# A transformer block in fp32 on one core: half of V made in the opening from unnormalised x, no V product inside attention, and the value differences made by GpSimd

## The chip, the core and the metric

The kernel runs on one core of a Trainium2 chip. The core has five engines that run side by side, each through its own list of instructions in order: TensorE (PE in the profile, its weight loads PEld), VectorE (DVE), ScalarE (ACT), GpSimd (POOL) and SyncE (SP), whose list here holds only transfers (SPq). ScalarE's list holds transfers too (ACTq). An instruction waits for the semaphores of those it depends on, and everything behind it on that engine waits with it. The metric is the device time of one execution in microseconds (us).

## The reference

The program is one layer (`DEPTH = 1`) on `x` of 1024 tokens by 1024 channels, all float32:

```python
mod = silu(c) @ ada_w + ada_b                 # six vectors of 1024: sh1, sc1, g1, sh2, sc2, g2
h = rmsnorm(x, ln1_g) * (1 + sc1) + sh1
q, k, v, cb, cc, cx, ga, gb = split(h @ w_in) # 8 sections of 1024 columns
q, k = rmsnorm per head of 64; 16 heads
y_a = stick_breaking_attention(q, k, v)       # strictly causal, no softmax
y_b = cb * causal_dwconv3(cc * cx)
merged = sigmoid(ga) * (y_a @ w_branch_a) + sigmoid(gb) * (y_b @ w_branch_b)
x = x + g1 * (merged @ w_out)
h = rmsnorm(x, ln2_g) * (1 + sc2) + sh2
x = x + g2 * ((silu(h @ w_gate) * (h @ w_up)) @ w_down)   # hidden width 2816
```

In the attention a weight is A[t,s] = sigmoid(z_ts) times the product over s<j<t of (1 - sigmoid(z_tj)). With P[t,s] the running product from the right, A[t,s] = P[t,s+1] - P[t,s], so the output is a sum of P against differences of neighbouring rows of v, plus the last row of v in the query block. That is how the kernel computes it: a scan for P, and products with v[s-1] - v[s].

For the change two facts matter. The norm of a token is one number r_t per row of x, so x's row can be multiplied by a weight matrix first and by r_t afterwards. And h = r_t * a * x + sh1 with a = ln1_g * (1 + sc1) per channel; the shift adds the same row sh1 @ W to every token's v. In differences of neighbouring rows that row cancels. It has to be put back only in the first difference and in the "last row" term.

## The kernel before

TensorE's matmuls take fp32r operands. For fp32 accuracy each operand is split into a high part (ScalarE copies it to fp32r) and a low part (VectorE subtracts), and each product is three matmuls: high x high, high x low, low x high. A "token" product (`mm_tok`) makes 128 tokens by 512 columns from 8 slices of 128 channels, that is 24 matmuls of 512 columns into one of 8 PSUM banks. Tiles in PSUM pools are called `pj` and `tr`, in later stages `e`.

The stages in order:

1. **Opening** (lines 165 to 350). The eight row tiles of `x` (`xq`) are loaded, squared and summed (odd ones by VectorE, even ones by ScalarE) and turned into r_t (`rstd_of`). TensorE meanwhile multiplies `xq` by the identity into a scratch bank (line 262, `warm`). The modulation's first two sections are dot products of 1024-wide rows of `ada` with silu(c), by VectorE (`mod_sum`, line 250, two per slice of 128 channels). r_t is spread over partitions by 8 small matmuls (`bcast`, line 279). Then, slice by slice, transposed `x` (`xts`) is normalised (`norm_x`, line 287), shifted and split (`make_hi` line 292, `make_lo` line 296), the weight split (`split_hi`, `split_lo`), and `real(k, ...)` issues slice k's 24 matmuls for 8 token tiles, which hold all 8 banks. This makes the first half of V (heads 0 to 7), stored in `d_v[0]`.
2. **K** (from line 430): 16 token tiles, with the factors of a Strassen scheme being made beside it (`factors`, `more`). Tiles `wpa` hold six 1024-wide weights; `raw` has two buffers.
3. **Gates** (from line 647): five sections by Strassen products. GpSimd makes sums of weights there.
4. **Attention** (from line 723). 16 heads by 8 query blocks give 128 steps. In each step TensorE makes scores (`z`, line 808), ScalarE the sigmoid, VectorE the scan (line 818); two steps later TensorE transposes (line 832), ScalarE and VectorE split (`ath` line 835, `atl` line 836), and three steps later TensorE multiplies by the value differences (`o`, lines 847 and 848). `att_dv` makes those for the next head: a difference on VectorE (tile `vb`), a high part on ScalarE, a low part on VectorE (tile `vt`). Between the steps TensorE runs fillers, paced by nominal costs (`F_Z`, `F_T`, `FILL`, `HEAD`): first the second half of V (lines 927 to 929, 2 x 8 tiles of 128 tokens by 256 columns), then the section cb (`C` below) and the product with `w_branch_b`, whose result VectorE multiplies by sigmoid(gb) (tile `mb`, line 982; sigmoid(gb) in tile `sgi`). `HEAD` = 16 pieces of filler come ahead of the first step. TensorE's instructions are chained in program order from the first step on, and so are attention's on VectorE.
5. **w_branch_a** (from line 1057): `ya` is loaded through `yr` (two buffers), split and multiplied; VectorE adds `mb`.
6. The output projection, the second norm, the FFN by Strassen products, as before and after.

In the opening every engine keeps program order, SyncE too (`in_order`); elsewhere a planner orders each engine's list, with attention's steps at high priority. The lines of the value difference:

```python
        if part == 0:
            tt(nc.vector, dv, dv, va[:, :, cs], ALU.subtract)
            return
        vt = vts[h] = bp.tile([P, KT, P], F32R, tag="vt", bufs=2, name=nm("vt"))
        nc.scalar.activation(vt[:, :, :DH], dv, AF.Copy)
        tt(nc.vector, vt[:, :, DH:], dv, vt[:, :, :DH].bitcast(F32), ALU.subtract)
```

Of the kernel before, what the change touches and what calls it, by code (L numbers as in the profile page):

```python
# [17 lines left out]
P = 128  # L18
# [12 lines left out]
def block_kernel(tc, x, x_t, cols, ada_1, ada_2, ada_row, w_q, w_kv, w_v1, w_cg, w_a, w_b, w_o, w_g, w_u, w_d, out):  # L31
# [38 lines left out]
    d_v = [drp.tile([n, P + 1, KT, P], F32, name=f"d_v{n}_{e}") for e, n in enumerate((4, 2, 2))]  # L70
# [5 lines left out]
    d_mb = drp.tile([KT, P, T], F32, name="d_mb")  # L76
    d_g = [drp.tile([P, D], F32, name=f"d_g{e}") for e in range(2)]
# [15 lines left out]
    nc.scalar.activation(one, one, AF.Sigmoid)  # L93
# [75 lines left out]
    sa_ = ExitStack()  # L169
    adp = sa_.enter_context(tc.tile_pool(name="adp", bufs=1, side="right", reuse_waits="tile"))  # L170
# [9 lines left out]
    xqs = [bigp.tile([P, 4, D], F32, tag="big", bufs=4, name=nm("xq")) for n in range(2)]  # L180
    xq = [xqs[i // 4][:, i % 4, :] for i in range(8)]
    rs = sp.tile([P, T], F32, name="rs")
    cab = sp.tile([P, D], F32, name="cab")
    nc.scalar.dma_start(cab, ada_row[0:1, :].broadcast_to([P, D]))
    hh = [big() for n in range(2)]
    junk = [h_[:, :2, :].rearrange("p a t -> p (a t)") for h_ in hh]

    def load_xq(i0_, i1_):
        for i in range(i0_, i1_):
            nc.sync.dma_start(xq[i], x[i * P:(i + 1) * P, :])  # L190
# [3 lines left out]

    wq = []
    MC0, MC = 3, 2
    ads = []

    def load_ada(e):
        ad = adp.tile([P, 2, D], F32, tag="ada", bufs=2, name=nm("ada")) if e % 3 < 2 else sp.tile(  # L200
            [P, 2, D], F32, tag="ada", bufs=1, name=nm("ada"))
        nc.sync.dma_start(ad, ada_1[e])
        ads.append(ad)
# [26 lines left out]

    load_xq(0, 4)
    load_ada(0)
    load_xq(4, 8)
    load_x(0)
    load_wq(0)
    load_ada(1)
    load_x(1)
    load_ada(2)
    load_x(2)
    load_wq(1)  # L240
    load_x(3)
# [4 lines left out]
    def mod_sum(e):  # L246

        msum = sp.tile([P, 2], F32, tag="msum", bufs=2, name=nm("msum"))
        for m in range(2):
            nc.vector.tensor_tensor_reduce(out=ads[e][:, m], in0=ads[e][:, m], in1=cab, scale=1.0, scalar=0.0, op0=ALU.mult,  # L250
                                           op1=ALU.add, accum_out=msum[:, m:m + 1])
# [84 lines left out]
    for k in range(KT - 1):  # L336
# [11 lines left out]
        if k % 2 == 0:  # L348
            load_wq(k // 2 + 2)
# [1279 lines left out]
```

## Time and profile before

| what | us |
|---|---|
| median of three runs | 1825.74 |
| lowest and highest run | 1823.97 and 1827.85 |
| profiled execution, its own time | 1827.39 |
| span of that execution, first to last instruction | 1825.6 |
| granted TensorE clock, mean over the span | 0.997 |
| TensorE busy | 1799.5 |
| VectorE busy | 1356.8 |
| ScalarE busy | 794.9 |
| GpSimd busy | 368.5 |

The page gives busy times by engine, the span in 40 slices, the chain of work that ended last, and groups of instructions. A row of a timeline is the start, the duration, the engine, the line of the kernel, the operation, what it writes and reads, how many instructions were merged, and in brackets how long the engine had been idle and what ended that. Matmuls are pipelined: a duration overlaps the next start, so the cost of one in a stream is read from the spacing of starts. A row of a window table gives each engine's busy time in a stretch, the number of its instructions, the granted clock and the use of the 16 DMA engines.

### The profile page before, as it was taken

The page shows a single profiled execution, that of the slowest core. Times are in us where ns is not written, and L with a number is a line of the kernel's source. Part 1 is how long each engine was busy: PE and PEld are TensorE (multiplying, and loading weights), DVE is VectorE, ACT ScalarE, POOL GpSimd, SP SyncE. Part 2 cuts the span into 40 slices and gives each one's busy share as a digit, 9 for nine tenths or more (in the row PEclk, how much of TensorE's full clock was granted, in tenths as well). Part 3 has the DMA queues.
Part 4 walks back from the last instruction along what each step waited for, and adds up shares of the span by engine and source line. Part 5 has one row for each costly group of instructions (what it writes and reads, how often), then busy time and mean ns, then how long its engine had stood idle before and what let it go on. Part 6 is the DMA issues. An engine that isn't in the chain of part 4 may idle for free.

```text
span 1825.6 us, 24915 instructions
## 1 busy us (share of the span) xinstructions
PE 1799.5 (99%) x8829; PEld 1502.2 (82%) x8829; DVE 1356.8 (74%) x1957; ACT 794.9 (44%) x1494; POOL 368.5 (20%) x277
## 2 busy tenths in 40 slices
PE   7999999999999999999999999999999999999999
PEld 5788778887879988888888788877888888878887
DVE  7873877779872899999887554689977888644776
ACT  3452653333343666666665221663444344322321
POOL 0043328323230000000000000115534544200000
PEclk9999999999999999999999999999999999999999
DMA  9687551227748566689654546324533344299766
GB/s 394 199 319 292 181 184 69 87 84 252 273 152 247 149 180 190 196 222 304 163 141 151 174 162 217 124 88 161 196 149 140 148 166 159 104 363 325 279 230 220
DMA packets 163508, 357.50 MB, mean 196 GB/s; under 512 B 15464, under 2 KB 60848, under 8 KB 161208
## 3 DMA queue, kind: packets, MB, share of 16 engines
q1 hardware_dynamic: 130920, 289.65, 47.5%
q10 hardware_dynamic: 31456, 62.59, 9.5%
q0 software_dynamic: 1008, 3.67, 0.5%
q8 instruction: 71, 1.16, 0.3%
q14 instruction: 53, 0.43, 0.1%
HBM read 245.22 MB, written 110.66 MB: 195 GB/s over the span
## 4 chain that ended last, share of the span: by engine, by line
PE 86%; DVE 7%; DMA 4%; issue 1%; ACT 1%; POOL 0%; SPq 0%; ACTq 0%; DVEq 0%; POOLq 0%
PE e L133 7%; PE e L132 7%; PE e L134 7%; PE pj L134 5%; PE pj L132 5%; PE pj L133 5%; PE pj L309 5%; PE pj L908 5%; PE pj L910 4%; PE pj L909 4%; PE e L1456 4%; PE e L1458 4%; PE e L1457 4%; PE tr L832 3%; PE o L848 2%; PE z L808 2%
## 5 line engine op out<-in xcount | busy, mean ns | idle before, releaser
L818 DVE TENSOR_TENSOR_SCAN pt<-pt,mk 128x128 f32<-128x128 f32 (+7 forms) x128 | 172.4, 1347 | 13.0 <-ACT pt L810 13.0
L132 PE MATMUL e<-big,whi 128*128 128x512 f32 x352 | 137.9, 392 | 2.0 <-DVE c L137 2.0
L133 PE MATMUL e<-big,whi 128*128 128x512 f32 x352 | 137.7, 391 | 0.0
L134 PE MATMUL e<-big,wlo 128*128 128x512 f32 x352 | 137.5, 391 | 0.0
L123 POOL TENSOR_SCALAR rs_m<-ss 128x1 f32<-128x1 f32 x8 | 2.3, 282 | 642.9 <-ACT xn L1259 642.9
L137 DVE TENSOR_TENSOR c<-e,c 128x512 f32<-128x512 f32 x138 | 92.8, 686 | 51.4 <-PE e L134 50.5
L132 PE MATMUL pj<-big,whi 128*128 128x512 f32 x320 | 125.2, 391 | 1.4 <-DVE c L137 1.4
L134 PE MATMUL pj<-big,wlo 128*128 128x512 f32 x320 | 124.8, 390 | 0.0
L133 PE MATMUL pj<-big,whi 128*128 128x512 f32 x320 | 124.6, 389 | 0.0
L1456 PE MATMUL e<-whi,f 128*128 128x512 f32 (+1 forms) x319 | 121.8, 382 | 1.1 <-DMA f<-d_f 1.1
L137 DVE TENSOR_TENSOR c<-pj,c 128x512 f32<-128x512 f32 x140 | 93.0, 681 | 38.9 <-PE pj L134 38.4
L1457 PE MATMUL e<-wlo,f 128*128 128x512 f32 (+1 forms) x319 | 121.8, 382 | 0.0
L1458 PE MATMUL e<-whi,f 128*128 128x512 f32 (+1 forms) x319 | 121.6, 382 | 0.0
L836 DVE TENSOR_TENSOR atl<-tr,ath 128x512 fp32r<-128x512 f32 (+1 forms) x192 | 103.9, 550 | 19.4 <-ACT ath L835 17.9
L810 ACT ACTIVATE pt<-z,rq 128x512 f32<-128x512 f32 (+1 forms) x192 | 104.7, 575 | 26.6 <-PE z L809 26.4
L908 PE MATMUL pj<-big,whi 128*128 128x512 f32 x256 | 114.0, 445 | 0.0
L309 PE MATMUL pj<-whi,big 128*128 128x512 f32 x352 | 109.3, 396 | 3.9 <-ACT big L292 3.9
L137 POOL TENSOR_TENSOR ws<-raw,raw 128x512 f32<-128x512 f32 x40 | 56.3, 1407 | 275.5 <-DMA raw<-w_cg 165.8
L137 DVE TENSOR_TENSOR wlo<-raw,whi 128x512 fp32r<-128x512 f32 x116 | 88.3, 766 | 31.6 <-ACT whi L463 31.0
L463 ACT ACTIVATE whi<-raw 128x512 fp32r<-128x512 f32 x116 | 72.4, 628 | 86.9 <-PE pj L133 45.4
L835 ACT ACTIVATE ath<-tr 128x512 fp32r<-128x512 f32 (+1 forms) x192 | 93.3, 487 | 30.0 <-PE tr L832 29.1
L133 PE MATMUL e<-rl,whi 128*128 128x512 f32 x264 | 102.8, 389 | 1.5 <-DVE rl L137 1.5
(258 smaller groups left out, 4998.6 us busy)
## 6 DMA issues: line engine op xcount, KB each, us to landing
f<-d_f SPq DMA_DIRECT2D x77, 512.0 KB, 4.3
d_f<-fs SPq DMA_DIRECT2D x70, 512.0 KB, 3.2
raw<-w_cg SPq DMA_DIRECT2D x40, 512.0 KB, 3.8
raw<-w_u SPq DMA_DIRECT2D x26, 512.0 KB, 3.2
raw<-w_g SPq DMA_DIRECT2D x25, 512.0 KB, 3.4
ad<-ada ACTq DMA_DIRECT2D x19, 512.0 KB, 4.5
ada<-ada SPq DMA_DIRECT2D x8, 1024.0 KB, 11.6
d_t<-ts SPq DMA_DIRECT2D x16, 512.0 KB, 3.7
```

The costliest lines, as they stand in the source:

```text
L132: nc.tensor.matmul(ps, wh[:, k, :], fh[:, k, :], start=(k == 0), stop=False)
L133: nc.tensor.matmul(ps, wh[:, k, :], fl[:, k, :], start=False, stop=False)
L134: nc.tensor.matmul(ps, wl[:, k, :], fh[:, k, :], start=False, stop=(k == 3))
L137: eng.tensor_tensor(out=out, in0=a, in1=b, op=op)
L309: nc.tensor.matmul(ps, a, b, start=(k == 0 and q == 0), stop=(k == KT - 1 and q == 2))
L810: nc.scalar.activation(pt[:, off + s0:off + s0 + m], z[:, :m], AF.Sigmoid, scale=rq[:, 1, i, h:h + 1])
L818: nc.vector.tensor_tensor_scan(out=pt[:, rev], data0=pt[:, rev], data1=mk[:, rev], initial=1.0, op0=ALU.mult, op1=ALU.max)
L836: nc.vector.tensor_tensor(out=tl[:, :nb, c0:c0 + P], in0=src, in1=th[:, :nb, c0:c0 + P].bitcast(F32), op=ALU.subtract)
L908: nc.tensor.matmul(ps, wh, rh_, start=(k == 0), stop=False)
L1456: nc.tensor.matmul(o, sh, w[0][:, c], start=(j == 0), stop=False)
L1457: nc.tensor.matmul(o, sh, w[1][:, c], start=False, stop=False)
L1458: nc.tensor.matmul(o, sl, w[0][:, c], start=False, stop=(j == NJ - 1))
```

## The change

Half of V moves from attention to the opening, and three smaller things go with it.

- The opening makes two passes. The first (`real(psr, k, ...)`) needs no norm: `raw_hi` and `raw_lo` split a * x, and the first half of V is built for six token tiles in step with the loads, for the last two in `tail`, out of the same slices. The evictions (`finish_raw`) multiply by r_t. `ada`'s two sections are loaded and reduced apart: the scale section (`scale_sum`) in the first pass, the shift section (`shift_sum`) in the second. The rows of x (`xq`) come later, through one ring of five buffers with `ada`, and ScalarE squares all eight. silu(c) is made by one row load, two matmuls with a row of ones and two activations. The second pass is the old one with the other 512 columns of V.
- The row sh1 @ W for the first half is made during the K stage: `shift_row` loads the four weights again and VectorE accumulates eight weighted slices; `put_row` reduces over partitions with two matmuls and stores the row to `d_v[0]` (negative) and `d_b`. `turn_vlast` adds it to the last rows.
- In attention the V filler is gone. The fillers are cb and w_branch_b only, cb in the order that the last tiles had before. `mb` is now copied out by ScalarE without sigmoid(gb). The pacing constants change (`F_S`, `FILL`, `HEAD` now 16 pieces of cb), and the first loads of attention are issued after two pieces of filler.
- In w_branch_a's stage sigmoid(gb) is loaded through the two `yr` buffers and GpSimd multiplies `mb` by it.
- `att_dv`'s two subtractions go from VectorE to GpSimd.

```diff
-    nc.scalar.activation(one, one, AF.Sigmoid)
+    nc.scalar.activation(one, one, AF.Silu)
...
-    nc.scalar.dma_start(cab, ada_row[0:1, :].broadcast_to([P, D]))
+    nc.scalar.dma_start(crow, ada_row[0:1, :])
...
+    def load_ring(src):
+        t = sp.tile([P, D], F32, tag="ld", bufs=NLD, name=nm("ld"))
+        nc.sync.dma_start(t, src)
+        return t
...
+    NLD, MC, NW, KB = 5, 2, 4, 2
...
+    def mod_dot(m, k):
+        ms = sp.tile([P, 1], F32, tag="msum", bufs=4, name=nm("msum"))
+        ad = ads.pop((m, k))
+        nc.vector.tensor_tensor_reduce(out=ad, in0=ad, in1=cab, scale=1.0, scalar=0.0, op0=ALU.mult, op1=ALU.add, accum_out=ms)
+        return ms
...
+    def square(i):
+        t = xq.pop(i)
+        nc.scalar.activation(t, t, AF.Square, accum_out=ss1[:, i:i + 1])
         if i % 4 == 3:
             rts.append(rstd_of(ss1[:, i - 3:i + 1], 1.0 / D, sp, 4, eng=nc.vector))
...
+    def raw_hi(k):
+        for n in range(2):
+            nc.scalar.activation(hh[n][:, k, :], xt(k, n), AF.Copy, scale=a1[:, k:k + 1])
+
+    def raw_lo(k):
+        for n in range(2):
+            nc.vector.scalar_tensor_tensor(out=hl[n][:, k, :], in0=xt(k, n), scalar=a1[:, k:k + 1],
+                                           in1=hh[n][:, k, :].bitcast(F32), op0=ALU.mult, op1=ALU.subtract)
...
+    def finish_raw(i):
+        vs = gw.tile([P, 512], F32, tag=("whi", "wlo")[i % 2], bufs=GS, name=nm("vs"))
+        r = rts[i // 4][:, i % 4:i % 4 + 1]
+        if i % 2:
+            nc.vector.tensor_scalar(out=vs, in0=psr[i], scalar1=r, scalar2=None, op0=ALU.mult)
+        else:
+            nc.scalar.activation(vs, psr[i], AF.Copy, scale=r)
+        store_v(vs, 0, i)
...
+    warm = ps_tr()
+    for e in range(2):
+        t = ps_pj()
+        nc.tensor.matmul(t, mk[0:1, D - P:], crow[:, e * 512:e * 512 + 512], start=True, stop=True)
+        nc.scalar.activation(cab[:, e * 512:e * 512 + 512], t, AF.Silu)
+    for e in range(NW):
+        nc.tensor.matmul(warm, ident, mk[:, 512:], start=True, stop=True)
+    scale_sum(0)
+    raw_hi(0)
+    split_hi(0)
+    scale_sum(1)
+    split_lo(0)
+    raw_lo(0)
+    split_hi(1)
+    NR = 6
+    psr = [ps_pj() for i in range(NR)] + [ps_tr() for i in range(8 - NR)]
+    for k in range(KT):
+        real(psr, k, range(MC), wq)
+        if k + 1 < KT:
+            raw_hi(k + 1)
+            split_lo(k + 1)
+        if k + 2 < KT:
+            scale_sum(k + 2)
+            split_hi(k + 2)
+        if k + 1 < KT:
+            raw_lo(k + 1)
+        real(psr, k, range(MC, NR), wq)
...
+    tail(0, KB)
+    for i in range(NR):
+        finish_raw(i)
+        if i == 1:
+            rsp = [ps_pj() for n in range(2)]
     bcast(0)
     bcast(1)
+    tail(KB, KT)
...
     for k in range(KT - 1):
-        mc = MC if k else MC0
-        real(k, 0, mc)
-        split_lo(k + 1)
+        real(pss, k, range(MC), wq[4:])
+        split_lo(k + 9)
...
+    def shift_row(j):
+        raw = g_raw(w_kv[0, j])
+        for k in (2 * j, 2 * j + 1):
+            r, sh = raw[:, k % 2 * 512:k % 2 * 512 + 512], mod[:, 0, k:k + 1]
+            if k == 0:
+                nc.vector.tensor_scalar(out=zb, in0=r, scalar1=sh, scalar2=None, op0=ALU.mult)
+            else:
+                nc.vector.scalar_tensor_tensor(out=zb, in0=r, scalar=sh, in1=zb, op0=ALU.mult, op1=ALU.add)
...
+        for e, t in enumerate(g_split(zb)):
+            nc.tensor.matmul(ps[:2], pm, t, start=(e == 0), stop=(e == 1))
...
-    F_Z, F_T, F_O = 0.2,0.3,0
+    F_Z, F_T, F_S = 0.2, 0.3, 0.05
...
-            tt(nc.vector, dv, dv, va[:, :, cs], ALU.subtract)
+            tt(nc.gpsimd, dv, dv, va[:, :, cs], ALU.subtract)
...
-        tt(nc.vector, vt[:, :, DH:], dv, vt[:, :, :DH].bitcast(F32), ALU.subtract)
+        tt(nc.gpsimd, vt[:, :, DH:], dv, vt[:, :, :DH].bitcast(F32), ALU.subtract)
...
-        yield F_Z
+        yield F_Z + F_S * ((i - 1) % 8 + 1)
...
-                    nc.tensor.matmul(ps, sh, wh, start=(k == 0), stop=False)
-                    nc.tensor.matmul(ps, sh, wl, start=False, stop=False)
-                    nc.tensor.matmul(ps, sl, wh, start=False, stop=(k == KT - 1))
...
-            nc.vector.tensor_tensor(out=mb, in0=ps, in1=sb, op=ALU.mult)
+            nc.scalar.activation(mb, ps, AF.Copy)
...
-    FILL = 2.5 * 16 * 5.2
+    FILL = 2.0 * 16 * 5.2
...
-    FILL -= 1.3 * HEAD
+    FILL -= 0.65 * HEAD
...
         for j in range(HEAD):
             next(fl)
+            if j == 1:
+                vl = load_vlast(0)
+                turn_vlast(0, vl)
+                att_load(0)
+                load_v(0, 1)
+                load_v(0, 0)
...
+        sb = fp.tile([P, 512], F32, tag="yr", bufs=2, name=nm("sgb"))
+        nc.sync.dma_start(sb, d_sgb[m, :, n * 512:(n + 1) * 512])
+        nc.gpsimd.tensor_tensor(out=mb, in0=mb, in1=sb, op=ALU.mult)
```

More of the change, by code (lines that the diff above doesn't have):

```diff
@@ L314, in block_kernel @@
-    make_hi(0, 0)
-    norm_x(0, 1)
-    make_hi(0, 1)
-    split_hi(1)
-    split_lo(0)
+    tail(KB, KT)
+    load_ada(0, 1)
+    load_ada(0, 2)
+    shift_sum(0)
+    for n in range(2):
+        norm_x(0, n)
+        make_hi(0, n)
     for n in range(2):
@@ L752, in load_v @@
         pr = h // 2
-        d = d_v[0][pr] if h < 8 else d_v[1 + (h - 8) // 4][pr % 2]
+        d = d_v[h // 8][pr % 4]
         t_ = ("vb", "va")[e]
```

233 lines of the change are left out of this document (106 added, 127 removed).

## The prediction

> **What bounds the kernel now.** I read the page first, then TensorE's waits, then windows by stage, then the timelines of the three places that the change touches. The rows of the waits are those of the stretches 0 to 130 us and 560 to 1020 us.
>
> ```profile
> PE 1799.5 (99%) x8829; PEld 1502.2 (82%) x8829; DVE 1356.8 (74%) x1957; ACT 794.9 (44%) x1494; POOL 368.5 (20%) x277
> ...
> PE pj L262 <- DMA xq<-x: 7.4, 3, 4.5
> PE pj L309 <- ACT big L292: 3.9, 8, 1.0
> ...
> PE pj L908 <- DVE mb L982: 1.7, 1, 1.7
> PE z L808 <- ACT pt L810: 0.4, 2, 0.2
> PE tr L832 <- DVE pt L818: 0.2, 1, 0.2
> ```
>
> TensorE is the bound nearly everywhere; outside the opening its longest wait in these stretches is 1.7 us. So work taken off it in attention counts in full, and work put on it elsewhere too, unless it falls into idle time. The idle time is in the opening:
>
> ```profile
> 0.00:21.80 21.80, 13.88 (x32) 6.05 (x33) 10.48 (x25) 8.78 (x15) 3.89 (x10) 0.92 0.93 365
> 21.80:72.00 50.20, 46.38 (x193) 35.42 (x194) 46.11 (x70) 19.26 (x34) 0.00 (x0) 1.00 0.66 264
> ...
> 100.00:170.00 70.00, 70.00 (x336) 57.69 (x335) 39.56 (x59) 27.01 (x45) 29.38 (x29) 1.00 0.86 332
> ...
> 577.00:997.30 420.30, 419.53 (x2653) 371.40 (x2652) 364.08 (x511) 267.59 (x605) 0.00 (x0) 1.00 0.69 192
> ```
>
> The columns are PE, PEld, DVE, ACT, POOL busy, then clock, DMA share, GB/s. Until 21.8 us TensorE does nothing useful but 16 small `bcast` matmuls; its identity products over `xq` are thrown away. From 21.8 to 72 us it makes one half of V and VectorE is 92% busy (46.11 of 50.20).
>
> ```profile
> 21.80 0.98 PE L309 MATMUL pj<-whi,big 128*128 128x512 f32 x3 [0.29 <-ACT big L292]
> ...
> 36.16 1.53 PE L309 MATMUL pj<-whi,big 128*128 128x512 f32 x6
> 37.53 0.62 PE L309 MATMUL tr<-whi,big 128*128 128x512 f32 x2
> ...
> 71.99 0.39 PE L309 MATMUL pj<-whi,big 128*128 128x512 f32 x1
> ```
>
> Six matmuls take 37.53 - 36.16 = 1.37 us, 0.228 each. V's 192 matmuls should take 43.8 us, and take 71.99 (the first of K) - 21.80 = 50.2: 6.4 us are lost beside the 21.8.
>
> **The V filler goes.** In attention the other half of V is 3 lines of 128 matmuls with 256 columns:
>
> ```profile
> L927 PE MATMUL pj<-whi,big x128: 277/283/365, 566.1 to 635.9; 128*128 128x256 f32 x128
> ...
> 573.21 0.28 PE L927 MATMUL pj<-whi,big 128*128 128x256 f32 x1
> ...
> 577.40 0.28 PE L929 MATMUL pj<-whi,big 128*128 128x256 f32 x1
> ```
>
> Between the last two rows lie 35 starts, so one costs 4.19 / 35 = 0.120 us, and 384 cost 46.0. All of it is on a TensorE that waits for nothing: **-46.0**, if VectorE can follow (below). Its splits, evictions and stores go too and were hidden.
>
> **The opening grows.** When can its first product start? A wait for `cst` ended at 4.64 us; the row `crow`, issued behind it, is taken to land with it.
>
> ```profile
> 4.64 0.15 DVE L109 TENSOR_SCALAR cst<-cst 128x1 f32<-128x1 f32 x1 [3.51 <-DMA cst<-cols]
> ...
> 4.55 2.05 PE L262 MATMUL pj<-xq,dm 128*128 128x512 f32 x2 [4.55 <-DMA xq<-x]
> ...
> 13.90 5.36 PE L262 MATMUL pj<-xq,dm 128*128 128x512 f32 x8 [2.25 <-DMA xq<-x]
> 19.10 1.05 PE L279 MATMUL tr<-dm,rs_r 128*128 128x128 f32 x8
> 20.35 1.16 PE L279 MATMUL tr<-dm,rs_r 128*128 128x128 f32 x8 [0.19 <-POOL rs_r L124]
> ```
>
> An fp32 matmul of 512 columns is two instructions: 2.05 us early on, 5.36 / 4 = 1.34 later. Two for silu(c) end at 4.6 + 4.1 = 8.7, four warm-up ones at 8.7 + 5.4 = 14.1. The other chain runs beside it: the second Silu (about 0.6) to 9.3, `scale_sum(0)` 1.2 and 0.2 to 10.7, two `raw_hi` 1.3 to 12.0, `split_hi(0)` to 12.6. I take 14.0 for the first product, between 11.5 (quick warm-ups, both chains short) and 17 (the first loads late).
>
> From there three engines race, slice by slice. The prices of the steps, from slice 1 of before:
>
> ```profile
> 24.14 1.22 DVE L250 CUSTOM_DVE_ANT_0 ada<-ada,cab 128x1024 f32<-128x1024 f32 x1
> ...
> 26.54 0.22 DVE L252 SCALAR_TENSOR_TENSOR a<-msum,acp,cst 128x1 f32<-128x1 f32 x1
> 26.85 1.28 DVE L287 SCALAR_TENSOR_TENSOR xts<-xts,a,rs 128x1024 f32<-128x1024 f32 x1
> 28.05 0.68 DVE L223 TENSOR_TENSOR wlo<-raw,whi 128x512 fp32r<-128x512 f32 x1
> 28.98 1.41 DVE L296 SCALAR_TENSOR_TENSOR big<-xts,mod,big 128x512 fp32r<-128x512 f32 x2 [0.25 <-ACT big L292]
> ...
> 28.23 1.34 ACT L292 ACTIVATE big<-xts,mod 128x512 fp32r<-128x512 f32 x2 [2.54 <-DVE xts L287]
> 29.47 0.62 ACT L218 ACTIVATE whi<-raw 128x512 fp32r<-128x512 f32 x1
> ...
> 14.05 1.04 ACT L267 ACTIVATE big<-xq 128x1024 fp32r<-128x1024 f32 x1
> ...
> 20.00:30.00 10.00, 8.34 (x38) 6.13 (x37) 8.83 (x14) 5.63 (x10) 0.29 (x1) 1.00 1.01 422
> ```
>
> Before, VectorE had two dot products, a norm, a weight split and `make_lo`: 2 x 1.22 + 0.22 + 1.28 + 0.68 + 1.41 = 6.0 us a slice against 24 x 0.228 = 5.5 on TensorE, which is the loss seen. In the first pass it has one dot product, no norm: 1.22 + 0.22 + 0.68 + 1.41 = 3.5, ScalarE 1.34 + 0.62 + a square of 1.04 and its read (0.2) = 3.2, against 18 x 0.228 = 4.1 on TensorE. Loads are 1.25 MB a slice, later 1.75 with `xq`: 3.0 to 4.1 us at 422 GB/s, and they have 14 us of start. SyncE keeps order, so a load that waits for a ring or `raw` buffer holds all behind it; those buffers are freed by VectorE's dot products and splits, which run ahead of TensorE by some slices, so this is costed at nothing. The second pass gives VectorE 1.22 + 1.28 + 0.68 + 1.41 = 4.6 against 5.5. So both passes go at TensorE's pace: 14.0 + 384 x 0.228 (87.6; both halves of V) + `bcast` 2.2 + some 0.6 of small gaps = 104.4 us. Between the passes the evictions, r_t and the first normalised slice (some 6 us on VectorE) lie beside `tail`'s last 36 matmuls (8.2 us). Against 72.0 before: **+32.4**, from +29.9 to +35.4 by the start alone.
>
> **The row of shifts, in the K stage.** Two matmuls, 0.5 us. Eight VectorE steps of about 0.74 and a split, 6.6 us, lie in a stage where VectorE was busy 39.56 of 70; 2 MB more loads meet a DMA share of 0.86 (5 us of it). K's own weight loads queue behind the four in the two `raw` buffers. **+0.5**, up to +3.
>
> **Attention's start.** The first scores came at 577.52 us, the next only at 591.56, since 23 us of V filler stood between.
>
> ```profile
> 577.52 0.22 PE L808 MATMUL z<-skh,sqt 128*128 128x128 f32 x1
> ...
> 591.56 0.28 PE L808 MATMUL z<-skh,sqt 128*128 128x256 f32 x1
> ```
>
> Now the head is 16 pieces of three matmuls, 48 x 0.228 = 10.9 us from 566.1, so scores are due at 577, about when the loads allowed them before; those loads now stand behind two pieces of filler and the loads of `cy`. Then steps follow with thin filler, and the first value difference needs two GpSimd steps. At best the 0.6 us of waits there vanish, at worst the loads come 8 us late. I take **+2**.
>
> **VectorE and GpSimd in attention.** TensorE's work from 566.0 to 997.3 us, where the products of w_branch_a begin, falls from 431.3 by 46.0 to 385.3; without the head's 11, 374 for the steps. VectorE's work:
>
> ```profile
> L137 DVE TENSOR_TENSOR vb<-vb,va 128x512 f32<-128x512 f32 x16 | 10.8, 672 | 0.8 <-DMA vb<-d_v 0.8
> ...
> L137 DVE TENSOR_TENSOR vt<-vb,vt 128x512 fp32r<-128x512 f32 x16 | 10.7, 671 | 0.0
> ...
> L982 DVE TENSOR_TENSOR mb<-pj,sgi x16: 664/690/692, 837.8 to 1008.2; 128x512 f32<-128x512 f32 x16
> ...
> L1118 DVE TENSOR_TENSOR wlo<-raw,whi x77: 677/693/1784, 1093.7 to 1589.1; 128x512 fp32r<-128x512 f32 x77
> ...
> L137 POOL TENSOR_TENSOR ws<-raw,raw x40: 1281/1296/2447, 139.7 to 1565.4; 128x512 f32<-128x512 f32 x40
> ```
>
> 364.1 - 10.8 - 10.7 - 11.0 (`mb`, 16 x 0.69) - 2.7 (four V splits) = 328.9, 88% of 374, against 364.1 of 420.3 = 87% before. ScalarE gets 16 x 0.6 = 10 us for `mb` and is far from full. GpSimd's 32 steps cost 1.3 us each where they meet nothing, and are due steps ahead of their use. But GpSimd and VectorE slow each other: in later stages, where both work, one and the same VectorE split goes from 0.69 to 1.78 us, one GpSimd sum from 1.30 to 2.45. If each of the 32 holds VectorE for 1.3 us, VectorE has 328.9 + 41.6 = 370.5 of 374, and unevenness costs TensorE up to 10 us; at nothing held it costs 0. About half of VectorE's work (the splits out of PSUM) can go on meanwhile, and before, VectorE at 87% made no wait, so I take **+1.5**.
>
> The Trainium skill, "SBUF — State Buffer", section "SBUF: two separate sides", says that a VectorE step with two SBUF inputs and a GpSimd step that reads SBUF exclude each other for a whole instruction. The two maxima above agree with that. By that rule the sum would take the upper end of this cost, 10 instead of 1.5 us, and come to 1824.5.
>
> **The handover to w_branch_a.** `mb`'s wait of 1.7 may go with ScalarE; sigmoid(gb) now waits for a `yr` buffer, in SyncE's order ahead of later loads. Its GpSimd product must be done before VectorE adds:
>
> ```profile
> 1007.41 0.33 SPq L1062 DMA_DIRECT2D yr<-d_ya  x1
> ...
> 1012.04 0.69 DVE L1084 TENSOR_TENSOR sgi<-sgi,mb 128x512 f32<-128x512 f32 x1
> ```
>
> The last `yr` load is issued at 1007.4, so sigmoid(gb) can follow about 1 us later, land in some 3 and be multiplied (1.3) by 1013: a microsecond late once, covered by two PSUM banks. **0**, from -1.7 to +4. One more table load on ScalarE (1.3 us, as at the start) has no one waiting.
>
> **The sum.** -46.0 + 32.4 + 0.5 + 2 + 1.5 + 0 = -9.6 us. The profiled execution took 1827.39 (span 1825.6), so 1817.8 there; the median is 1825.74, 1.65 lower: **1816**.
>
> **The rivals.**
> *A, the opening is fed late.* Squares or loads come behind and `finish_raw`, which needs all of r_t, holds the banks between passes. For it: eight squares on ScalarE, the last after a ring of five. Against: the DMA moved 422 GB/s. A stop of 6 us: 1822.
> *B, attention's start stalls.* The head no longer covers loads and latency: 8 instead of 2 us, 1822.
> *C, slower: GpSimd holds VectorE.* The place is attention's 32 steps. TensorE's pace breaks beyond 374 - 328.9 = 45 us of held time; a loss over the remaining 11.1 (9.6 + 1.5) needs 56 us, 1.75 per step. Against it: a GpSimd step takes 1.3 us alone, and held for that in full the time is 1816 - 1.5 + 10 = 1824.5, no slower than before. For it: the 2.45 us above. At 2 us, 64 are held, 19 beyond: 1816 - 1.5 + 19 = 1833.
> *D, the change does not do what it says:* the filler was only cover. VectorE's 56 idle us (420.3 - 364.1) are waits that stay, and attention falls to 328.9 + 56 = 385, not 374: +11, 1826. Against: TensorE hardly waits there (2.3 us), so its own work sets the pace.
>
> **Chances.** Forecast 0.48, A 0.13, B 0.12, C 0.17, D 0.10. Faster by over 0.2% (3.65 us, about what a measurement can tell) is 0.73, the same 0.10, slower 0.17. The likeliest alone has 1809 to 1821. For eight in ten I leave out a tenth on each side, cutting through C: 1808 to 1830.
>
> **What would show it.** First useful product at about 14 us, K's first matmul near 104; no 256-column products writing `pj` in attention; 385 to 390 us from the end of the gates to the end of attention; TensorE's waits there under 5 us. Wrong would be: TensorE waits for `pt` or `atl` in attention with VectorE above 95%, or a gap between the two passes.

## The result, and the profile after

The changed kernel takes **1835.38 us** (median of 4 runs, 1832.57 to 1837.05) beside 1826.12 us (4 runs, 1823.97 to 1827.85) for the kernel before: ratio 1.0054, 95% interval 1.0039 to 1.0068. The forecast was 1816, with a range up to 1830. The change is slower, by some 9 us, and the forecast was wrong in sign. One execution of run e10 below took 2226.15 us at a granted clock of 0.754 and is left out of its median; all other executions here stand at a clock of 0.990 or more.

The profiled execution of the changed kernel took 1836.08 us (span 1834.3). TensorE is still busy nearly all the time, with 194 matmuls fewer. First the busy row of its page:

```profile
PE 1800.1 (98%) x8635; PEld 1491.4 (81%) x8635; DVE 1346.5 (73%) x1932; ACT 815.3 (44%) x1527; POOL 439.9 (24%) x325
```

The windows cut the span at the same places in both kernels: first useful product, K, attention (its first filler), the first product of w_branch_a, the first of the output projection. The columns are PE, PEld, DVE, ACT, POOL busy, then clock, DMA share, GB/s. After:

```profile
14.73:104.04 89.31, 89.31 (x402) 74.04 (x401) 64.14 (x99) 44.86 (x77) 2.06 (x2) 1.00 0.66 238
104.04:600.80 496.76, 491.66 (x2203) 401.59 (x2202) 363.54 (x539) 195.77 (x325) 184.33 (x128) 1.00 0.56 195
600.80:998.60 397.80, 390.61 (x2364) 334.83 (x2363) 338.66 (x456) 266.51 (x602) 49.96 (x32) 1.00 0.69 190
998.60:1099.90 101.30, 93.93 (x409) 76.75 (x408) 49.15 (x72) 24.28 (x43) 21.11 (x16) 0.97 0.56 186
1099.90:1834.30 734.40, 725.00 (x3255) 600.46 (x3253) 525.92 (x753) 277.44 (x471) 180.56 (x139) 1.00 0.54 193
```

Before (its opening was shown in the prediction):

```profile
72.00:566.10 494.10, 490.66 (x2201) 401.48 (x2200) 362.86 (x528) 195.32 (x323) 183.47 (x128) 1.00 0.54 194
566.10:997.30 431.20, 430.43 (x2748) 382.15 (x2747) 364.08 (x511) 269.84 (x611) 0.00 (x0) 1.00 0.70 195
997.30:1090.80 93.50, 91.79 (x410) 75.81 (x409) 46.77 (x71) 24.48 (x41) 0.00 (x0) 1.00 0.48 168
1090.80:1825.60 734.80, 726.36 (x3254) 601.31 (x3252) 526.51 (x753) 277.25 (x471) 181.17 (x139) 1.00 0.53 192
```

| stage | before | after | difference | forecast |
|---|---|---|---|---|
| to K's first matmul | 72.0 | 104.0 | +32.0 | +32.4 |
| K and gates | 494.1 | 496.8 | +2.7 | +0.5 |
| attention | 431.2 | 397.8 | -33.4 | -42.5 (46.0 less, 2 and 1.5 more) |
| w_branch_a | 93.5 | 101.3 | +7.8 | 0 |
| the rest | 734.8 | 734.4 | -0.4 | 0 |

They add up to the 8.7 us between the spans. So the loss has two places: attention wins 9 us less than forecast, and the stage of w_branch_a, which was to cost nothing, costs 8. TensorE's waits of the changed kernel name both; these are five of its rows. The columns are the wait and what ended it, us in total, times, the longest:

```profile
PE pj L1000 <- DVE sgi L1147: 6.6, 2, 6.1
...
PE tr L924 <- DVE pt L910: 3.1, 3, 1.4
...
PE z L900 <- DMA skh<-d_k: 1.5, 1, 1.5
...
PE o L939 <- POOL vt L138: 1.2, 1, 1.2
PE z L901 <- DMA skl<-d_k: 0.8, 1, 0.8
```

**The stage of w_branch_a.** The 6.1 us wait is the last link of a chain, here in the timelines of SyncE, GpSimd, ScalarE, VectorE and TensorE (start, duration, what, and in brackets the idle time before it and its releaser):

```profile
1080.84 0.32 SPq L1143 DMA_DIRECT2D sgb<-d_sgb  x1
1081.25 0.38 SPq L1107 DMA_DIRECT2D raw<-w_o  x1
...
1087.96 0.33 SPq L1107 DMA_DIRECT2D raw<-w_o  x1
...
1079.53 1.28 POOL L1144 TENSOR_TENSOR mb<-mb,sgb 128x512 f32<-128x512 f32 x1 [5.83 <-DMA mb<-d_mb]
...
1084.90 1.15 ACT L1111 ACTIVATE whi<-raw 128x512 fp32r<-128x512 f32 x2 [8.12 <-DMA raw<-w_o]
...
1073.62 1.28 DVE L1112 TENSOR_TENSOR wlo<-raw,whi 128x512 fp32r<-128x512 f32 x2
...
1085.56 2.37 DVE L1112 TENSOR_TENSOR wlo<-raw,whi 128x512 fp32r<-128x512 f32 x2 [4.80 <-ACT whi L1111]
...
1091.40 0.69 DVE L1112 TENSOR_TENSOR wlo<-raw,whi 128x512 fp32r<-128x512 f32 x1 [1.48 <-ACT whi L1111]
1092.01 0.68 DVE L1147 TENSOR_TENSOR sgi<-pj,sgi 128x512 f32<-128x512 f32 x1
...
1092.75 0.80 PE L1000 MATMUL pj<-ya,whi 128*128 128x512 f32 x1 [6.11 <-DVE sgi L1147]
```

The gate tile `sgb` has two buffers. Its load for a later group stands in SyncE's list and waits until GpSimd has multiplied an earlier one (1079.53 + 1.28 = 1080.81; the load leaves at 1080.84). Everything behind it waits too, and right behind it is a load that has nothing to do with the gate: the preload of w_out, which comes in three pieces through one buffer `raw`. The second piece could have left when VectorE had split the first, at 1073.62 + 1.28 = 1074.90; it leaves at 1081.25, 6.4 us late. The third needs the same buffer and leaves as soon as the second is split (1085.56 + 2.37 = 1087.93; it leaves at 1087.96). VectorE keeps order, and the product that frees TensorE's bank (1092.01) stands behind the split of the third piece (1091.40). In the kernel before, the second piece leaves at once when the first is split (1069.81 + 1.28 = 1071.09):

```profile
1071.13 0.33 SPq L1046 DMA_DIRECT2D raw<-w_o  x1
...
1069.81 1.28 DVE L1051 TENSOR_TENSOR wlo<-raw,whi 128x512 fp32r<-128x512 f32 x2
```

**Attention.** Most of the idle time there is in the first 40 us. Windows and TensorE's timeline, after:

```profile
610.00:615.00 5.00, 2.84 (x18) 1.75 (x16) 0.21 (x1) 0.22 (x1) 0.00 (x0) 1.00 1.14 240
615.00:620.00 5.00, 4.84 (x18) 4.12 (x19) 1.61 (x4) 2.05 (x5) 1.88 (x2) 0.66 1.14 288
620.00:625.00 5.00, 3.06 (x18) 2.30 (x17) 5.00 (x5) 3.65 (x8) 3.36 (x3) 1.00 1.13 260
```

```profile
614.05 0.30 PE L900 MATMUL z<-skh,sqt 128*128 128x128 f32 x1 [1.51 <-DMA skh<-d_k]
615.16 0.40 PE L901 MATMUL z<-skl,sqt 128*128 128x128 f32 x1 [0.81 <-DMA skl<-d_k]
...
624.33 0.39 PE L939 MATMUL o<-ath,vt 128*128 128x256 f32 x1 [1.21 <-POOL vt L138]
```

The key tile is late, and the clock falls to 0.66 in the 5 us behind that wait. Then VectorE is full (5.00 of 5.00) while GpSimd works too. Those are the candidates: late loads, a head too short to cover them, and GpSimd holding VectorE.

### The profile page after: what moved, and what is told of

The parts are those of the page before. It is cut to its first block, busy times and chain, and to the rows that moved or that the text cites. A ratio compares the mean times of both kernels' runs of the same rounds, so it can differ in the third digit from the quotient of the medians.

```text
span 1834.3 us, 24591 instructions
## 1 busy us (share of the span) xinstructions
PE 1800.1 (98%) x8635; PEld 1491.4 (81%) x8635; DVE 1346.5 (73%) x1932; ACT 815.3 (44%) x1527; POOL 439.9 (24%) x325
## 3 DMA queue, kind: packets, MB, share of 16 engines
q8 instruction: 69, 1.13, 0.3%
## 5 line engine op out<-in xcount | busy, mean ns | idle before, releaser
L910 DVE TENSOR_TENSOR_SCAN pt<-pt,mk 128x128 f32<-128x128 f32 (+7 forms) x128 | 177.0, 1383 | 5.1 <-ACT pt L902 5.1
L294 PE MATMUL pj<-whi,big 128*128 128x512 f32 x448 | 132.8, 393 | 0.0
L133 PE MATMUL pj<-big,whi 128*128 128x512 f32 x320 | 125.4, 392 | 2.6 <-DVE c L138 2.6
L134 PE MATMUL pj<-big,whi 128*128 128x512 f32 x320 | 124.6, 389 | 0.0
L1000 PE MATMUL pj<-big,whi 128*128 128x512 f32 x256 | 114.3, 446 | 0.0
L135 PE MATMUL e<-rh,wlo 128*128 128x512 f32 x264 | 102.7, 389 | 0.0
L133 PE MATMUL e<-rh,whi 128*128 128x512 f32 x264 | 102.7, 389 | 0.0
L1001 PE MATMUL pj<-big,whi 128*128 128x512 f32 x256 | 101.4, 396 | 0.0
```

The source lines that it names most:

```text
L133: nc.tensor.matmul(ps, wh[:, k, :], fh[:, k, :], start=(k == 0), stop=False)
L134: nc.tensor.matmul(ps, wh[:, k, :], fl[:, k, :], start=False, stop=False)
L135: nc.tensor.matmul(ps, wl[:, k, :], fh[:, k, :], start=False, stop=(k == 3))
L294: nc.tensor.matmul(ps, a, b, start=(k == 0 and q == 0), stop=(k == KT - 1 and q == 2))
L910: nc.vector.tensor_tensor_scan(out=pt[:, rev], data0=pt[:, rev], data1=mk[:, rev], initial=1.0, op0=ALU.mult, op1=ALU.max)
L1000: nc.tensor.matmul(ps, wh, rh_, start=(k == 0), stop=False)
```

## The experiments

The comparisons are with the kernel before on the same chip, whose median was 1825.2 to 1827.1 us from one set of runs to the next; so the ratio says more than the median. The theories that the expectations name: **H**, the handover to w_branch_a costs 8 to 10 us; **S**, attention's start is short of cover; **L**, GpSimd's steps hold VectorE (the prediction's rival C). Each block of code shows the changed lines that matter; "..." stands for the code between them.

**e1: the gate product back in the filler, on VectorE.**

```diff
 # filler of w_branch_b
...
+            sb = sbs.pop(0) if sbs else load_sb(m, n)
...
-            nc.scalar.activation(mb, ps, AF.Copy)
+            nc.vector.tensor_tensor(out=mb, in0=ps, in1=sb, op=ALU.mult)
...
 # stage of w_branch_a
-        sb = fp.tile([P, 512], F32, tag="yr", bufs=2, name=nm("sgb"))
-        nc.sync.dma_start(sb, d_sgb[m, :, n * 512:(n + 1) * 512])
-        nc.gpsimd.tensor_tensor(out=mb, in0=mb, in1=sb, op=ALU.mult)
```

> The gate product goes back to where the kernel before had it: VectorE multiplies branch b's result by its gate as it leaves the accumulator, and the stage of w_branch_a loads neither the gate nor asks GpSimd for anything. The changed kernel took 101.3 us from the first w_branch_a product to w_out's first, the kernel before 93.5. Theory H (the handover): the gate's loads and GpSimd's product are what made the stage longer, so it falls back to 93.5 to 94.5, the 6.1 us wait for the product with branch a's gate is gone, and the time is 1827 to 1829. Theory L (GpSimd holds VectorE throughout attention): this edit leaves GpSimd's subtractions alone and puts 16 products of 0.69 us back on VectorE, so the time stays at 1835 or rises to 1838. Theory S (the loss sits at attention's start): as L, attention itself keeps its 397.8 us; only what H claims may move.

Measured 1825.53 us, ratio 1.0002 (0.9994 to 1.0011). The stage of w_branch_a took 1093.5 - 1000.7 = 92.8 us and TensorE's only wait in it was 1.1 us. H holds, and gives more than it promised.

**e2: four gate buffers, the product still on GpSimd.**

```diff
-        sb = fp.tile([P, 512], F32, tag="yr", bufs=2, name=nm("sgb"))
+        sb_pool, sb_tag = ((fp, "yr"), (wx, "sgb"))[nsgb % 2]
+        nsgb += 1
+        sb = sb_pool.tile([P, 512], F32, tag=sb_tag, bufs=2, name=nm("sgb"))
```

> The product stays on GpSimd in the stage of w_branch_a; its gate tiles get four buffers (two of the ones it had and two in the right-hand pool) in place of two. Theory H1 (SP's order: each gate load waits in SP's queue for the product two groups earlier, and everything behind it waits too, the preload of w_out among it): the gate loads stand ready, w_out's second preload leaves by 1076 and not at 1081 us of the old trace, the 6.1 us wait goes, and the stage falls to 94 to 96 us, the time to 1828 to 1830. Theory H2 (GpSimd's product itself is late, or holds VectorE at the end of each group): buffers do not help, the stage stays at 100 us and the time at 1834 to 1836.

Measured 1825.78 us, ratio 1.0003 (0.9992 to 1.0014), the same as e1. SyncE's and VectorE's timelines:

```profile
1068.89 0.33 SPq L1107 DMA_DIRECT2D raw<-w_o  x1
...
1066.49 2.38 DVE L1112 TENSOR_TENSOR wlo<-raw,whi 128x512 fp32r<-128x512 f32 x2
...
1072.93 1.29 DVE L1112 TENSOR_TENSOR wlo<-raw,whi 128x512 fp32r<-128x512 f32 x2 [0.87 <-ACT whi L1111]
```

The second piece of the preload again leaves at once when the first is split (1066.49 + 2.38 = 1068.87, against 1068.89), not 6.4 us late; it leaves 12.4 us earlier than in the changed kernel, of which 5.2 us are that the stage itself began earlier in this execution. VectorE waits 0.87 us for it and not 4.80, and the stage takes 1085.7 - 993.4 = 92.3 us. So the cause is not where the product is made, but that its operand had two buffers and its load stood in one list with everybody's loads. H1 is shown, H2 falls.

**e3: the two subtractions of the value differences back on VectorE.**

```diff
-            tt(nc.gpsimd, dv, dv, va[:, :, cs], ALU.subtract)
+            tt(nc.vector, dv, dv, va[:, :, cs], ALU.subtract)
...
-        tt(nc.gpsimd, vt[:, :, DH:], dv, vt[:, :, :DH].bitcast(F32), ALU.subtract)
+        tt(nc.vector, vt[:, :, DH:], dv, vt[:, :, :DH].bitcast(F32), ALU.subtract)
```

> The two subtractions of the value differences go back to VectorE; all else as in the changed kernel. Theory L (GpSimd's 16 steps hold VectorE in attention, and the loss of some 10 us there is theirs): attention falls from 397.8 to 388 to 390 us and the time to 1826 to 1828. Theory S (the loss is at attention's start, where TensorE waits for late key loads and for the first scans): VectorE, full for 20 us there, gets some 2.3 us of work more, and the time is 1834 to 1838. If the subtractions cost nothing on either engine, 1835.

Measured 1835.64 us, ratio 1.0052 (1.0039 to 1.0066): no change. Taken alone this would have buried L. But attention did fall, from 397.8 to 995.2 - 600.1 = 395.1 us, and the stage behind it gave it back (104.7 us, where it had been 101.3), by the same wait:

```profile
PE pj L1000 <- DVE sgi L1147: 9.6, 3, 8.0
```

Whether L is worth anything can't be read while the handover sets the end. e7 and e8 ask again.

**e7: both repairs, four gate buffers and the subtractions on VectorE** (the edits of e2 and e3).

> Four gate buffers as in e2, and the two subtractions of the value differences on VectorE as in e3, where attention took 395.1 us against 397.8 and the stage after it gave the 2.7 us back. Theory L: with that stage mended the gain reaches the end, 1822.5 to 1824. Theory N (where the subtractions run does not matter to the end): 1825 to 1827.

Measured **1820.00 us**, ratio 0.9964 (0.9950 to 0.9978). This is faster than both kernels. Between e2 (1.0003) and e7 lie 0.39%, 7 us; the two medians are 5.8 us apart. The two profiled executions don't show this: they took 1822.15 us (e2, its fastest of 1822.15 to 1831.67) and 1822.19 (e7, its slowest of 1818.42 to 1822.19), and attention 397.0 and 395.1. The size of this price therefore rests on the repeated runs, and only its kind on the traces. The other comparison is with e3: the same four buffers, with the subtractions on VectorE, are worth 1.0052 less 0.9964, 16 us, and not the 9 to 10 that they are worth in e2. So the two repairs depend on each other.

**e8: the kernel before, with only the two subtractions moved to GpSimd** (e3's edit the other way round).

> The kernel before with one part of the change alone: the two subtractions of the value differences on GpSimd. Theory L (16 steps of 1.3 to 4.1 us that hold VectorE, full at 83% in attention): VectorE's scans beside them take about as long again, attention grows by 3 to 10 us, 1829 to 1836. Theory N: it takes some 15 us of work off VectorE, which isn't the bound, and costs what the scans beside it lose in places with slack: 1825 to 1827. A gain, 1820 to 1824, if VectorE's full stretches were what TensorE waited for.

Measured 1833.71 us, ratio 1.0036 (1.0023 to 1.0049), 6.6 us slower. L holds: this one part alone costs the old kernel 6.6 us. In its trace attention took 1006.6 - 566.8 = 439.8 us beside 431.2, with 4.9 us of waits beside 0.6. How it does so can be seen in one place of e8, in the timelines of GpSimd, VectorE and TensorE and two windows:

```profile
749.21 1.29 POOL L137 TENSOR_TENSOR vt<-vb,vt 128x512 fp32r<-128x512 f32 x1 [23.72 <-ACT vt L767]
755.13 3.99 POOL L137 TENSOR_TENSOR vb<-vb,va 128x512 f32<-128x512 f32 x2 [4.63 <-issue]
...
755.60 2.44 DVE L818 TENSOR_TENSOR_SCAN pt<-pt,mk 128x768 f32<-128x768 f32 x1
757.96 1.71 DVE L137 TENSOR_TENSOR wlo<-raw,whi 128x512 fp32r<-128x512 f32 x1
...
764.84 0.66 PE L832 MATMUL tr<-dm,pt 128*128 128x128 f32 x4 [1.29 <-DVE atl L836]
```

```profile
763.00:766.00 3.00, 1.71 (x15) 1.45 (x13) 3.00 (x6) 1.67 (x5) 0.00 (x0) 1.00 1.08 228
766.00:769.00 3.00, 3.00 (x12) 2.68 (x11) 2.49 (x2) 0.19 (x1) 0.00 (x0) 0.50 1.18 213
```

Two GpSimd steps take 3.99 us, where a lone one takes 1.29. Beside them a weight split on VectorE takes 1.71 instead of 0.68. Five microseconds later, with VectorE full (3.00 of 3.00 in the window), TensorE waits 1.29 us for a split out of PSUM, and then its clock is at half for three microseconds (0.50), which costs another 1.5. In between, from 754.99 to 768.5 us, VectorE has almost no gap, so what it lost beside GpSimd it could not make up. This place explains about 3 of the 6.6 us. Another 2.5 us of e8's waits (0.42, 0.34 and 1.71) fall between 591 and 596 us, where no GpSimd step runs (one ends at 587.70, the next starts at 597.81); there ScalarE's splits wait for late weight loads, and no run shows whether GpSimd has a part in that. VectorE's scans over the whole of attention are longer wherever the subtractions are on GpSimd; here before, e8, after and e7 (count, total us and mean ns, idle before):

```profile
L818 DVE TENSOR_TENSOR_SCAN pt<-pt,mk 128x128 f32<-128x128 f32 (+7 forms) x128 | 172.4, 1347 | 13.0 <-ACT pt L810 13.0
```

```profile
L818 DVE TENSOR_TENSOR_SCAN pt<-pt,mk 128x128 f32<-128x128 f32 (+7 forms) x128 | 176.7, 1380 | 13.0 <-ACT pt L810 13.0
```

```profile
L910 DVE TENSOR_TENSOR_SCAN pt<-pt,mk 128x128 f32<-128x128 f32 (+7 forms) x128 | 177.0, 1383 | 5.1 <-ACT pt L902 5.1
```

```profile
L910 DVE TENSOR_TENSOR_SCAN pt<-pt,mk 128x128 f32<-128x128 f32 (+7 forms) x128 | 172.6, 1348 | 3.7 <-ACT pt L902 3.7
```

**e11: both moves to GpSimd undone** (e1's edit and e3's).

> The changed kernel with both moves to GpSimd undone: the gate product back in the filler (e1) and the two subtractions back on VectorE (e3). What is left of the change is the opening, the values without a filler, and the weight of the scans in the plan. If the two prices simply add (10 us and some 6 us below the changed kernel's 1835.4): 1819 to 1821, as e7. If VectorE, which then has all of its old work in an attention that is 46 us of filler shorter, becomes what TensorE waits for: 1823 to 1828.

Measured 1821.82 us, ratio 0.9984 (0.9976 to 0.9993). This lies between the two expectations. If both prices added in full, 1835.4 less 10 less 6, it would be 1819.4; with the gate product on VectorE the subtractions cost only 3.3 to 3.7 us (e1 to e11, by ratios and by medians), where they cost 5.8 to 7.1 with the product on GpSimd (e2 to e7). Why, no run shows. What is left of the change (the opening, the values without a filler) is a small gain. Beside e7 the gate product on GpSimd with four buffers is no worse than on VectorE; the two intervals just touch.

**Attention's start: e4, e5, e6, e9, e10, e12.** All of them try to win back the first 40 us. e4 puts attention's first loads ahead of the first filler; the others stand on e2 (e5, e6) or e7 (e9, e10, e12) and lengthen the head.

```diff
 # e4: the five lines from load_vlast(0) to load_v(0, 0) moved from "if j == 1:" to ahead of the loop
 # e5: HEAD = 32     e6: HEAD = 64
-    HEAD, TAIL = 16, 10.0
+    HEAD, TAIL = 32, 10.0
 # e9: HEAD = 24, e10: HEAD = 32, and the y tiles of the first three products loaded ahead of everything
+        ys = [load_y(m, n) for m, n in order[:3]]
...
+            y = ys.pop(0) if ys else load_y(m, n)
 # e12: HEAD = 32, and attention's first 14 loads issued by GpSimd
+        dq = nc.gpsimd if h < 2 else nc.sync
```

> Attention's first loads stand ahead of the first filler again, as in the kernel before; the number of fillers at the head stays 16. Theory S1 (the key tile of the first head was issued behind the filler's own loads, at 602 to 609 us of the trace, and TensorE reached its scores at 614): the two waits for the key halves (1.5 and 0.8 us) go, the clock dip behind them goes, attention falls by 3 to 6 us, and the time is 1829 to 1832. Theory S2 (what is short is the cover: 16 pieces of 0.65 us where the kernel before had 16 of 1.3): the loads cannot be issued before the stage ahead frees the room, so they move by 2 us at most, and the waits for scans and value tiles that follow stay: 1833 to 1835. Theory L: no change, 1835.

> Four gate buffers as in e2, and 32 pieces of the filler ahead of attention in place of 16 (20.8 us of TensorE's time by the plan's own count, as much as the kernel before put there). Theory S2 (what is lost in attention is lost in its first 40 us, because the head is half as long while the loads take as long): the waits for the key halves (1.4 and 0.8 us), for the first value tile (1.4) and for scans (2.1) fall under 2 us together, the clock stays at 1.00 there, attention falls from 397.0 to 389 to 391 us, and the time is 1818 to 1820 (e2 took 1825.8). Theory R (the loss is spread over attention, or the filler's removal was worth less than 46 us): attention stays within 2 us of 397 and the time is 1824 to 1826.

> As e5 with 64 pieces ahead. Theory S2: nothing is left to win at the start, and 32 pieces fewer stand beside the later scans; attention takes as long as with 32 or up to 5 us more where VectorE is full, 1818 to 1825. Theory R: 1824 to 1830. If with 32 the wait for the key tile was only shortened, 64 wins another 1 to 2 us.

> On e7 (four gate buffers, the subtractions on VectorE; 1820.0 us): the y tiles of the filler's first three products are loaded ahead of attention's first loads, and 24 pieces stand at the head. In e5 the head of 32 pieces removed the waits at attention's start, but TensorE stood 8.9 us for the product with a y tile that was queued behind attention's loads. Theory S2: with the y tiles there first, neither wait is left; 5 to 7 us of waits and lowered clock in attention's first 40 us go, attention falls from 395.1 to 388 to 391 us, and the time is 1813 to 1817. If the three loads push attention's own back by as much as the longer head covers, 1819 to 1821. If SP's order makes another product wait, as in e5: 1825 to 1830.

> As e9 with 32 pieces. Three y tiles are all that the three buffers hold, so the fourth is still queued behind attention's loads. Theory S2 with the y tile as the whole of e5's loss: 1813 to 1818, at most 2 us from e9. If the fourth y tile makes its product wait: 3 to 8 us above e9.

> On e7 (1820.0 us; attention 395.1), with a head of 32 pieces, and the loads of attention's first two heads (14 of them) issued by GpSimd, which has nothing else to do there, in place of SP. In e5, e9 and e10 the longer head took the waits for key and value tiles away, and a wait of 4 to 9 us for something queued on SP behind those loads came in their place: a y tile, or the store that frees the filler's output tile. Theory Q (SP's order at attention's start is what costs): nothing of the filler is behind the loads any more, TensorE waits under 2 us in attention's first 40, attention falls to 388 to 391 and the time is 1813 to 1817. Theory R (the start is short of something else, VectorE's time or the transfers themselves): attention stays at 394 to 397 and the time at 1819 to 1826. If loads issued by GpSimd are slower to arrive than by SP, the wait for the key tile returns even behind 20 us of filler: 1825 to 1835.

| run | median us | ratio, 95% interval | attention, us | its longest wait of TensorE |
|---|---|---|---|---|
| e4 | 1846.54 | 1.0113 (1.0098 to 1.0129) | 404.2 | 11.0 for a product with `cy` |
| e5 | 1832.98 | 1.0041 (1.0025 to 1.0057) | 405.4 | 8.9 for a product with `cy` |
| e6 | 1835.08 | 1.0045 (1.0030 to 1.0059) | 410.2 | 8.9 for a product with `cy` |
| e9 | 1825.04 | 1.0001 (0.9993 to 1.0010) | 396.9 | 4.5 for a sigmoid |
| e10 | 1828.67 | 1.0021 (1.0013 to 1.0030) | 399.0 | 3.8 for a sigmoid |
| e12 | 1826.73 | 1.0013 (1.0002 to 1.0024) | 396.7 | 2.6 for a sigmoid |

None beats what it was built on, and none reached the time that theory S or Q gave it; e4, e5 and e6 are slower than every case that was expected. In e5 the longer head took the waits for the key and value tiles away (no `skh`, `skl` or `vt` among its waits), and put a longer one in their place. TensorE's timeline of e4 and of e5:

```profile
625.64 0.80 PE L1000 MATMUL pj<-big,whi 128*128 128x512 f32 x1 [10.96 <-DVE cy L1017]
```

```profile
622.03 0.79 PE L1000 MATMUL pj<-big,whi 128*128 128x512 f32 x1 [8.93 <-DVE cy L1017]
```

The filler's y tiles stand in SyncE's list behind attention's loads; a filler that comes early needs them early (in e5 VectorE waits 4.24 us for the transfer of `cy`, in e4 9.35). In e9, where they come first, the next one in the list is late, the store that frees the filler's output tile. ScalarE's and TensorE's timelines of e9:

```profile
623.40 0.63 ACT L1027 ACTIVATE ybh<-cy 128x512 fp32r<-128x512 f32 x1 [5.95 <-DMA d_yb<-ybh]
623.94 0.93 ACT L902 ACTIVATE pt<-z,rq 128x512 f32<-128x512 f32 x2
...
624.66 0.80 PE L900 MATMUL z<-skh,sqt 128*128 128x512 f32 x1 [4.50 <-ACT pt L902]
```

ScalarE keeps order, so attention's sigmoid waits behind the filler's copy. In e12 attention's first loads are out of SyncE's list, and the same wait is still there, 2.6 us, with the clock down around it:

```profile
618.00:628.00 10.00, 7.42 (x29) 5.63 (x28) 7.97 (x14) 4.00 (x9) 0.00 (x0) 0.76 1.04 371
```

So theory Q, SyncE's order alone, falls, and S is half right: the start is short of cover, but more of this filler was no cover in any of the five runs that lengthened the head, and in e5, e9 and e12 what TensorE waits for hangs on a load or a store that the filler brings. The DMA share is 1.04 there, and it was 1.13 to 1.14 in the changed kernel. But in the kernel before it was 1.00 to 1.18 too, from 570 to 595 us, and TensorE waited 0.6 us in all. So full transfers alone do not bring the waits, and that they are the last limit there was not tested by itself.

## Why the prediction was wrong, step by step

**The handover to w_branch_a: the largest failure.** The step said "a microsecond late once", 0, with 4 as its upper end. It costs 9 to 10 us (1.0054 against 1.0002 and 1.0003): in the stage's trace 5.7 us more of waits, and 1.7 us of clock behind the longest (0.50 from 1093 to 1096 us, 0.94 to 1100). The step looked at the first group alone, and there it was right: VectorE waits 1.00 and 0.69 us for GpSimd's product in the first two groups, and TensorE does not wait for it. It never counted the steady state: one more load per group in SyncE's list, each tied by two buffers to a GpSimd step two groups earlier. It had named the ingredient ("waits for a `yr` buffer, in SyncE's order ahead of later loads") without asking what the later loads were. One of them is the preload of w_out.

**VectorE and GpSimd in attention: mis-sized.** I took 1.5 us, out of 0 to 10; the runs say 3 to 7 (e8: 6.6; e2 to e7: 5.8 by medians and 7.1 by ratios; e1 to e11: 3.7 and 3.3). The argument for the small end was that VectorE at 87% made no wait before, so a little more would make none either. But the load is not spread: VectorE is full for 10 us and more at a time, and one GpSimd pair that stretches a scan and a split by a microsecond or less each inside such a stretch reaches TensorE. The Trainium skill, "SBUF — State Buffer", section "SBUF: two separate sides", by which the sum would have taken 10 us, was nearer than the estimate from rows for e8 and for e2 to e7, and not for e1 to e11. The traces agree with its rule: a scan and a split with two SBUF operands grow (1.71 for 0.68), and GpSimd's own pair grows with them (3.99).

Rival C had the mechanism with a chance of 0.17, but its size was wrong the other way: its 1833 needed 19 us held beyond VectorE's slack, and alone it would have ended at 1816 - 1.5 + 6.6 = 1821. The changed kernel was not slower by C alone, but by C and the handover together. The prediction's sign of being wrong, waits for `pt` with VectorE above 95%, came true at attention's start (4.94 to 5.00 of each 5 us from 620 to 640, with waits of 0.73 and 1.42 us for `pt`). But e7 has such waits too, 4.0 us, with no GpSimd step in attention, so they are no proof of C.

**The V filler goes: right in kind.** Attention fell by 33.4 us with GpSimd's steps in it, by 36.1 in e7 (431.2 - 395.1). TensorE's waits in e7's attention sum to 6.8 us (4.0 + 1.6 + 0.8 + 0.4) where before they were under 1, and the clock dips behind the wait for the key tile. That dip is worth 1.7 us in the changed kernel (5 us at 0.66) and in e7 (3 us at 0.68 and 3 at 0.75). So of the 9.9 us between 46.0 and 36.1, some 6 are waits and 2 the clock; the rest has no row of its own and stays open.

**Attention's start: mis-sized.** I took +2, between -0.6 and +8. It measured 8.5 in the changed kernel and in e7, if all the waits of attention and the lowered clock are put down to it (6.8 + 1.7). Rivals B (8 us) and D ("the filler was only cover") were nearer: the removed filler needed no y tile and little of VectorE, and it stood between the first scores and the next. The prediction says for 23 us; its two rows show 14.0 (577.52 to 591.56). D's mechanism is there at most in part: its 11 us would have been time in which TensorE waits, and TensorE is idle for 7.2 of attention's 397.8 us, 5.9 of them from 610 to 640 us. Seven arrangements of the start (the change, e4, e5, e6, e9, e10, e12) all leave TensorE waiting 6 us or more in attention.

**The opening grows: right.** First product at 14.73 (forecast 14.0), K's first matmul at 104.04 (104.4), with no gap between the passes: TensorE is busy for 89.31 of 89.31 us. Rival A, an opening fed late, did not happen.

**The row of shifts: not decided.** K and gates took 2.7 us longer. But the first filler came anywhere from 595.7 to 601.1 us in the profiled executions of the experiments on the changed kernel (e8 stands on the one before), whose code is the same up to there except for a few early loads, so 2.7 is inside what one execution differs from another.

Put together: forecast 1816, with 10 instead of 0 for the handover and 3.3 to 6.6 instead of 1.5 for GpSimd, gives 1828 to 1831. The 4 to 8 us that are left are of the size of attention's waits and clock, 8.5 less the 2 taken. That term stands apart from the other two: without GpSimd's steps 1814.5 was to be expected, and e7, with the handover repaired as well, took 1820.0. Without the first two, e7 and e11 took 1820.0 and 1821.8, a gain of 3 to 7 us over the kernel before.

## What to carry to other kernels

When a change adds a load to a stage, write down for each group which buffer it waits for, and what stands behind it in the same list: the price is not the load, but the unrelated transfer that it holds up. When work leaves a full engine for a second one, look at that engine's full stretches and not at its share; two more SBUF readers beside a scan are not free. And an experiment that undoes one part can show nothing because another part sets the end (e3); undo both before calling a part harmless.

## What the runs showed of the hardware

A short wait of TensorE can cost about twice its length. In e8 a single wait of 1.29 us was followed by three microseconds at half clock, 1.5 us more; in the changed kernel waits of 1.51 and 0.81 us in a row were followed by 5 us at 0.66. I had counted such waits at their own length. But other waits as long were followed by none: in the changed kernel the clock stays at 1.00 from 620 to 650 us, with waits of 1.21 and 1.42 us in that stretch, and in the kernel before it stays at 1.00 behind a wait of 1.71 us at 1009.04. What decides which wait is followed by a dip, these traces do not show. The Trainium skill, "TensorE: Matmul & The Clock Gate", section "What's actually happening", puts the fall of the clock after an idle window of about 3.4 us; here 1.29 us of one wait was enough once, and the measurement decides.

A GpSimd step and a VectorE step that meet, both with two operands in SBUF, are both longer: 3.99 us for two GpSimd steps that take 2.56 alone (e8, 582.64 us), and 1.71 for a VectorE split that takes 0.68 alone; VectorE's split out of PSUM beside such a pair kept its time (0.53 us for 384 columns in the changed kernel). GpSimd's and VectorE's timelines of the changed kernel:

```profile
622.59 4.12 POOL L138 TENSOR_TENSOR vt<-vb,vt 128x512 fp32r<-128x512 f32 x2 [1.64 <-ACT vt L853]
...
623.13 0.53 DVE L928 TENSOR_TENSOR atl<-tr,ath 128x384 fp32r<-128x384 f32 x1
623.58 2.04 DVE L910 TENSOR_TENSOR_SCAN pt<-pt,mk 128x640 f32<-128x640 f32 x1
...
743.99 1.48 DVE L910 TENSOR_TENSOR_SCAN pt<-pt,mk 128x640 f32<-128x640 f32 x1
```

The scan of 640 columns reads two SBUF operands and took 2.04 us beside the pair and 1.48 away from any.
